# A two-layer decoder trunk on one core: column units and down steps of the FFN laid out anew

## The chip, the cores and the metric

The kernel runs on one core of one Trainium2 chip. The metric is the device time of one execution in microseconds (us); lower is better. One core has five engines that are spoken of below: PE (TensorE, matrix products), DVE (VectorE), ACT (ScalarE), POOL (GpSimd) and SP, which here only issues DMA transfers, in the order in which they are written. Each engine works through its own instructions in order and waits on semaphores for the others.

## The reference

Two layers over a stream of 1024 tokens by 1024 features, all in float32. Layer 0 is a gated DeltaNet mixer, layer 1 a stick-breaking attention; each is followed by the same feed-forward network (FFN), and it is in the FFN that the change lies:

```
def swiglu(x, w_gu, w_down):
    g, u = jnp.split(x @ w_gu, 2, axis=-1)
    return (jax.nn.silu(g) * u) @ w_down

for layer in range(DEPTH):                       # DEPTH = 2, D_FF = 2816
    hn = rms_norm(h, attn_norm[layer])
    h = h + (gdn_mixer if layer == 0 else sb_mixer)(hn, ...)
    h = h + swiglu(rms_norm(h, ffn_norm[layer]), w_gu[layer], w_down[layer])
```

## The kernel before

The program runs the mixer of layer 0 (to about 700 us), its FFN (to about 1430), the attention (to about 1930) with its output projection, and the second FFN (from about 1975 to the end). Both FFNs are made by one function, `ffn`.

**Precision and products.** Every float32 operand is held as two parts, hi (the value cast by ACT) and lo (the rest, by a DVE subtraction); `parts_of` makes both (L359 the cast, L360 the subtraction). A product is then three matmuls (`triple`, L450 hi by hi, L451 hi by lo, L452 lo by hi). On top of that the FFN multiplies 2x2 blocks with seven products instead of eight, which needs sums and differences of blocks on both sides and of the results. The seven products of an item are numbered 1 to 7, and `Seven.steps` runs one.

**Column units.** The 2816 hidden columns are 22 units of 128. A unit's left sides are its gate and up weights; its right sides are the normed activations X, kept by `PairNorm` as four column blocks (j = 0 to 3) under the names 11, 21, 22, T1 to T4. `PairNorm.half` makes 11 and 21 from the first half of the tokens; `second(j)` makes T1 = second-half row minus raw, and T2 from it, each with its parts (two ACT copies L407, two DVE subtractions L408 and L409, then `parts`); `side5`, `side347` and `side4` make T1's parts, T3 and 22, and T4's parts later. The units' results are combined by `c11`, `u2`, `u3`, `c21`, `c12` (L525 to L549; L537 is ACT's copy in `u3`, L548 the Silu and L549 POOL's last multiply).

**Pairs and DRAM.** Two units make a pair (11 pairs, q = 0 to 10). `sums(q)` forms the pair's left sides for the down projection: four POOL sums (L578, L579, L582, L583), hi by ACT and lo by DVE (L586, L587, and L558, L559 in `split_put`), and stores them to DRAM, `hsa[q]` and `hsb[q]`, by `put` (L552). It is a generator that is advanced once at every product step of PE.

**Down steps.** 24 blocks, four (row groups c) for each of six groups gi; group 0 is pair 0 alone and takes four plain products (11, 21, 12, 22), the others two pairs and seven products. A block reads its left sides back from DRAM by `hid_load` (hA from `hsa` into four buffers of tag w, L664 for group 0, L669 else; hB from `hsb`, L676). `Right` makes a pair's right sides from `w_down`: `load` (L630, three raw buffers), `sums` (POOL, L638 to L641), `split` (parts). `rows_load` fetches the residual rows h (L682). What is done beside each product is set by hand in `beside_unit` and `beside_block`; the numbers of the steps there (s, k) are the order of the work. Results go into h by L718.

Of the kernel before, what the change touches and what calls it, by code (L numbers as in the profile page):

```python
# [18 lines left out]
P = 128  # L19
# [4 lines left out]
def yoco_kernel(  # L24
# [338 lines left out]
    class PairNorm(Norm):  # L363
# [36 lines left out]
        def second(self, j):  # L400

            rr = [x_tile(F32), x_tile(F32)]
            t1 = x_tile(F32)
            t2 = x_tile(F32) if j < 3 else main.tile([P, HB], F32, tag="og", name="t2")
            for k, r in enumerate(rr):
                kt = 4 * k + j
# [4 lines left out]
            self.tt = getattr(self, "tt", []) + [(*rr, t1, t2)]  # L411

        def side5(self, j):
            self.parts("T1", j, self.tt[j][2])

        def side347(self, j):
            r12, r22, _, t2 = self.tt[j]
            dve.tensor_tensor(r12, r22, r12, op=ALU.subtract)
            self.parts("T3", j, r12)
            dve.tensor_tensor(t2, self.raw[4 + j], t2, op=ALU.subtract)  # L420
            self.parts("22", j, r22, self.x2)

        def side4(self, j):
            self.parts("T4", j, self.tt[j][3])
# [29 lines left out]
    def ffn(norm, rows, w_gu, w_down, hp, done, after=None, sizes=(1, 2, 2, 2, 2, 2)):  # L454
# [119 lines left out]
        def sums(q):  # L574

            v = [hid.pop(2 * q + k) for k in range(2)]
            s = W()
            pool.tensor_tensor(s[:, 0], v[0][:, :, 1], v[1][:, :, 1], op=ALU.add)  # L578
            pool.tensor_tensor(s[:, 1], s[:, 0], v[0][:, :, 0], op=ALU.subtract)  # L579
            yield  # L580
            v3, v4 = v[0][:, :, 1], main.tile([P, 4, P], F32, tag="og", name="s4")
            pool.tensor_tensor(v3, v[0][:, :, 0], v3, op=ALU.subtract)  # L582
            pool.tensor_tensor(v4, v[1][:, :, 0], s[:, 1], op=ALU.subtract)  # L583
# [4 lines left out]
            yield  # L588
            yield
            for k in range(2):  # L590
                put(hsa[q], 2 + k, hi[:, k].bitcast(F32))
                put(hsa[q], 6 + k, s[:, k])
            yield from split_put(hsa[q], 0, 4, *(t[:, :, 0] for t in v))
            yield
            yield
            yield from split_put(hsb[q], 0, 3, v3, v[1][:, :, 1])
            yield
            yield from split_put(hsb[q], 2, 5, v4)
            yield
# [19 lines left out]
        class Right:  # L619


            def __init__(self, gi, q):
                self.gi, self.q, self.w = gi, q, {}
                wd[gi][q] = self.w

            def load(self):
                self.r = [raw_tile([P, 2, HB]) for _ in range(2)]
                for k in range(2):
                    r0 = (2 * self.q + k) * P
                    sp.dma_start(self.r[k].rearrange("p a b -> p (a b)"), w_down[r0 : r0 + P, :])  # L630
# [134 lines left out]
        def beside_unit(i, s):  # L765
# [47 lines left out]
        def beside_block(b, s):  # L813
            gi, c = divmod(b, 4)
            if gi == 0:
                k = 6 + 4 * (c - 1) + s if c else s
                if k == 2:
                    pend.append(sums(NPAIR - 1))
                if s == 0:
                    if c < 3:  # L820
                        rows_load(c + 1)
                    hid_load(b + 1)
                if k == 0:
                    right(1, 0, "split", 7)
                elif k == 1:
                    right(1, 0, "split", 3, 4)
                    right(1, 1, "load")
                elif k == 3:
                    right(1, 1, "sums")
                elif k in (5, 7, 9, 11, 13, 15, 16):  # L830
# [44 lines left out]
        u2.split_g()  # L875
        run_.step(0, 6)
        for j in range(4):
            norm.side5(j)
        run_.step(1, 6)
        for u, k in ((u0, 0), (u1, 1)):  # L880
            u.c11(run_.bank[k, "A"])
        u0.split34()
        run_.step(2, 1)
        run_.step(0, 5)
        u1.split34()
        for j in range(4):
            norm.side347(j)
# [839 lines left out]
```

## Time and profile before

| | us |
|---|---|
| runs | 2680.41, 2686.52, 2685.96 |
| median of the runs | 2685.96 |
| profiled execution, its own time | 2682.77 |
| its span in the profile | 2681.0 |
| granted TensorE clock, mean | 0.987 |

The profiled execution is the one whose rows are shown below. Its time is 1.8 us more than its span, and 3.2 us less than the median of the three runs. Busy time counts an engine's instructions; PE's matmuls overlap, so PE is told best by when one starts after the other. A group of waits names the instruction that waited and the one that released it last. Line numbers are those of the kernel before.

### The profile page before, as it was taken

The page shows a single profiled execution, that of the slowest core. Times are in us where ns is not written, and L with a number is a line of the kernel's source. Part 1 is how long each engine was busy: PE and PEld are TensorE (multiplying, and loading weights), DVE is VectorE, ACT ScalarE, POOL GpSimd, SP SyncE. Part 2 cuts the span into 40 slices and gives each one's busy share as a digit, 9 for nine tenths or more (in the row PEclk, how much of TensorE's full clock was granted, in tenths as well). Part 3 has the DMA queues.
Part 4 walks back from the last instruction along what each step waited for, and adds up shares of the span by engine and source line. Part 5 has one row for each costly group of instructions (what it writes and reads, how often), then busy time and mean ns, then how long its engine had stood idle before and what let it go on. Part 6 is the DMA issues. An engine that isn't in the chain of part 4 may idle for free. (4 is left out here: it accounts for less than half of the span.)

```text
span 2681.0 us, 35748 instructions
## 1 busy us (share of the span) xinstructions
PE 2550.9 (95%) x12908; PEld 2078.1 (78%) x12908; DVE 1820.2 (68%) x2715; ACT 1143.9 (43%) x2207; POOL 825.1 (31%) x1248
## 2 busy tenths in 40 slices
PE   8999999999989999979999999999899999996999
PEld 6777877877768888857777778887777888885777
DVE  6666776675685666657755788778668566664874
ACT  6333333343463444432215666667545444442220
POOL 2444444443401222234313333332410221223420
PEclk9999999999999999989999999999999999998999
DMA  4222222222423554477661111111333445547765
GB/s 121 65 62 57 55 65 53 72 92 72 145 84 109 169 157 143 144 245 276 232 216 63 40 32 32 40 40 63 111 118 102 128 142 163 164 143 258 244 230 200
DMA packets 368374, 331.75 MB, mean 124 GB/s; under 512 B 19507, under 2 KB 320702, under 8 KB 368198
## 3 DMA queue, kind: packets, MB, share of 16 engines
q1 hardware_dynamic: 368198, 329.48, 38.8%
q8 instruction: 101, 1.65, 0.2%
q14 instruction: 75, 0.61, 0.1%
HBM read 226.37 MB, written 103.06 MB: 123 GB/s over the span
## 5 line engine op out<-in xcount | busy, mean ns | idle before, releaser
L140 PE MATMUL ups<-x,wh 128*128 128x512 f32 (+1 forms) x912 | 388.7, 427 | 0.0
L142 PE MATMUL ups<-x,wl 128*128 128x512 f32 (+1 forms) x912 | 363.6, 399 | 0.0
L141 PE MATMUL ups<-x,wh 128*128 128x512 f32 (+1 forms) x912 | 359.7, 395 | 0.0
L450 PE MATMUL ips<-x,w 128*128 128x512 f32 x840 | 328.1, 392 | 15.3 <-ACT x L359 9.3
L451 PE MATMUL ips<-x,w 128*128 128x512 f32 x840 | 328.7, 391 | 2.7 <-DVE x L360 2.5
L452 PE MATMUL ips<-x,w 128*128 128x512 f32 x840 | 327.9, 390 | 0.0
L549 POOL TENSOR_TENSOR n<-n,ev 128x512 f32<-128x512 f32 x44 | 68.8, 1564 | 695.3 <-ACT n L548 695.3
L450 PE MATMUL ups<-x,w 128*128 128x512 f32 x648 | 253.6, 393 | 1.7 <-ACT x L359 1.7
L451 PE MATMUL ups<-x,w 128*128 128x512 f32 x648 | 253.8, 392 | 0.0
L452 PE MATMUL ups<-x,w 128*128 128x512 f32 x648 | 253.2, 391 | 0.0
L142 PEld LDWEIGHTS ups<-x,wl 128*128 128x128 f32 (+1 forms) x912 | 170.9, 187 | 37.5
L450 PEld LDWEIGHTS ips<-x,w 128*128 128x128 f32 x840 | 157.4, 188 | 53.3 <-ACT x L359 11.9
L140 PEld LDWEIGHTS ups<-x,wh 128*128 128x128 f32 (+1 forms) x912 | 172.2, 189 | 22.7
L141 PEld LDWEIGHTS ups<-x,wh 128*128 128x128 f32 (+1 forms) x912 | 172.2, 189 | 21.2
L451 PEld LDWEIGHTS ips<-x,w 128*128 128x128 f32 x840 | 157.9, 188 | 37.7 <-DVE x L360 4.9
L452 PEld LDWEIGHTS ips<-x,w 128*128 128x128 f32 x840 | 158.0, 188 | 32.9
L718 DVE TENSOR_TENSOR h<-h,ips 128x512 f32<-128x512 f32 x176 | 119.4, 683 | 68.8 <-PE ips L452 68.8
L450 PEld LDWEIGHTS ups<-x,w 128*128 128x128 f32 x648 | 122.5, 189 | 28.7 <-ACT x L359 3.3
L451 PEld LDWEIGHTS ups<-x,w 128*128 128x128 f32 x648 | 122.5, 189 | 26.8 <-DVE x L360 1.6
L452 PEld LDWEIGHTS ups<-x,w 128*128 128x128 f32 x648 | 122.2, 189 | 25.4
L718 DVE TENSOR_TENSOR h<-h,ups 128x512 f32<-128x512 f32 x136 | 92.7, 682 | 58.4 <-PE ups L452 58.3
L360 DVE TENSOR_TENSOR w<-raw,w 128x1024 fp32r<-128x1024 f32 (+1 forms) x88 | 101.0, 1163 | 40.8 <-DMA hsb<-w 31.5
(351 smaller groups left out, 5935.5 us busy)
## 6 DMA issues: line engine op xcount, KB each, us to landing
raw<-in_ffn_w_gu_dram SPq DMA_DIRECT2D x88, 512.0 KB, 3.9
w<-hsa SPq DMA_DIRECT2D x88, 512.0 KB, 4.2
hsa<-w SPq DMA_DIRECT2D x128, 256.0 KB, 2.8
hb<-hsb SPq DMA_DIRECT2D x72, 384.0 KB, 4.1
raw<-in_ffn_w_down_dram SPq DMA_DIRECT2D x44, 512.0 KB, 3.8
raw<-in_gdn_w_in_dram SPq DMA_DIRECT2D x32, 512.0 KB, 4.1
hsb<-w SPq DMA_DIRECT2D x60, 256.0 KB, 3.7
hsa<-n SPq DMA_DIRECT2D x48, 256.0 KB, 3.6
```

The costliest lines, as they stand in the source:

```text
L140: pe.matmul(o, wh[:, kt, :m], xh, start=kt == 0, stop=False)
L141: pe.matmul(o, wh[:, kt, :m], xl, start=False, stop=False)
L142: pe.matmul(o, wl[:, kt, :m], xh, start=False, stop=kt == KT - 1)
L360: dve.tensor_tensor(lo, src, hi, op=ALU.subtract)
L450: pe.matmul(ps, ah, bh, start=start, stop=False, skip_group_check=True)
L451: pe.matmul(ps, ah, bl, start=False, stop=False, skip_group_check=True)
L452: pe.matmul(ps, al, bh, start=False, stop=stop, skip_group_check=True)
L549: pool.tensor_tensor(s, s, self.t3, op=ALU.mult)
L718: dve.tensor_tensor(d, d, ps, op=ALU.add)
```

## The change

Four things change, in `PairNorm` and `ffn`.

- **Start-up.** `second(j)` takes t1 and t2 straight from PSUM by two DVE instructions that multiply by the gain and subtract (new L406, L407). Of the two ACT copies only that of the row block 22 (`r22`) is left. T3 is formed as t2 minus raw, in a tile of its own. `behind` is the last lo part of T2 (new L411), and `issue_after` orders on DVE everything from u2's split to `side347` behind it; `u1.split34` moves between the columns of `side347`.
- **Pair sums.** `sums(q)` casts and subtracts its halves apart (512 wide) and stores hi, lo, hi, lo. For the last pair its tiles are ten small ones, its lo subtractions are POOL's instead of DVE's (new L602), and it begins four steps later (k = 6 instead of 2).
- **Loads.** The right sides' halves are loaded apart and earlier; `hid_load` for blocks 0 to 4 and `rows_load` move to other steps, so that those of blocks 0 to 3 stand ahead of the last pair's stores. In block 4 the load for block 5 moves from s = 1 to s = 5.
- **Splits.** Group 1's first pair is split in another order (5 and 7 later by a step, 3 and 4 too).

```diff
 def second(self, j):
-    rr = [x_tile(F32), x_tile(F32)]
...
-        act.activation(r, self.columns(self.hn, kt), AF.Copy, scale=self.gain[:, kt : kt + 1])
-    dve.tensor_tensor(t1, rr[0], self.raw[j], op=ALU.subtract)
-    dve.tensor_tensor(t2, rr[1], t1, op=ALU.subtract)
-    self.parts("T2", j, t2)
+    p12, p22 = self.columns(self.hn, j), self.columns(self.hn, 4 + j)
...
+    dve.scalar_tensor_tensor(t1, p12, g(j), self.raw[j], op0=ALU.mult, op1=ALU.subtract)
+    dve.scalar_tensor_tensor(t2, p22, g(4 + j), t1, op0=ALU.mult, op1=ALU.subtract)
+    act.activation(r22, p22, AF.Copy, scale=g(4 + j))
+    hi, lo = x_tile(), x_tile()
+    act.copy(hi, t2)
+    self.behind = dve.tensor_tensor(lo, t2, hi, op=ALU.subtract)

 def side347(self, j):
-    dve.tensor_tensor(r12, r22, r12, op=ALU.subtract)
-    self.parts("T3", j, r12)
+    t3 = x_tile(F32)
+    dve.tensor_tensor(t3, t2, self.raw[j], op=ALU.subtract)
+    self.parts("T3", j, t3)

 def sums(q):
-    s = W()
+    last = q == NPAIR - 1
+    w = None if last else W()
+    s = [small(), small()] if last else [w[:, 0], w[:, 1]]
...
-    hi = mw()
-    act.copy(hi, s)
-    dve.tensor_tensor(s, s, hi, op=ALU.subtract)
+    for n, (dst, k0, k1, srcs) in enumerate(todo):
+        if last:
+            his = [small(F32R) for _ in srcs]
...
+        for hi, src in zip(his, srcs):
+            act.copy(hi, src)
+            (pool if last else dve).tensor_tensor(src, src, hi, op=ALU.subtract)
...
+        for k, (hi, src) in enumerate(zip(his, srcs)):
+            put(dst, k0 + k, hi.bitcast(F32))
+            put(dst, k1 + k, src)

 def beside_unit(i, s):
-    if i == NF - 2 and s == 6:
-        right(0, 0, "load")
+    if i == NF - 2 and s in (1, 6):
+        right(0, 0, "load", int(s == 6))
     if i == NF - 1:
         if s == 0:
+            right(1, 0, "load", 0)
+        elif s == 1:
             right(0, 0, "sums")
             right(0, 0, "split", 11, 12)
         elif s == 2:
             right(0, 0, "split", 21, 22)
-            right(1, 0, "load")
+            right(1, 0, "load", 1)
+        elif s == 3:
+            rows_load(0)
         elif s == 4:
             hid_load(0)
-            rows_load(0)
             right(1, 0, "sums")
         elif s == 5:
+            hid_load(1)
             right(1, 0, "split", 1, 2)
         elif s == 6:
-            right(1, 0, "split", 6, 5)
+            rows_load(1)
+            right(1, 0, "split", 6)

 def beside_block(b, s):
-        if k == 2:
-            pend.append(sums(NPAIR - 1))
-        if s == 0:
-            if c < 3:
-                rows_load(c + 1)
-            hid_load(b + 1)
         if k == 0:
+            hid_load(2)
+            right(1, 0, "split", 5)
+        elif k == 1:
             right(1, 0, "split", 7)
-        elif k == 1:
+            right(1, 1, "load")
+        elif k == 2:
+            rows_load(2)
+            hid_load(3)
             right(1, 0, "split", 3, 4)
-            right(1, 1, "load")
         elif k == 3:
             right(1, 1, "sums")
+        elif k == 6:
+            rows_load(3)
+            pend.append(sums(NPAIR - 1))
+        elif k == 10:
+            hid_load(4)
...
-        if s == 1:
+        if s == (5 if b == 4 else 1):
             hid_load(b + 1)

+with tc.issue_after(norm.behind.ins):
     u2.split_g()
...
```

**What moves, first place: DVE at the start-up** (first FFN; x, t and w are tiles of activations, of t2 and of weights). Before, from the first column's L408 on:

```order
L408 TENSOR_TENSOR x<-x,x_7517 128x512
L360 TENSOR_TENSOR w<-w 128x1024
L409 TENSOR_TENSOR x<-x 128x512
L360 TENSOR_TENSOR w<-w 128x1024
L418 TENSOR_TENSOR x<-x 128x512
L360 TENSOR_TENSOR x<-x 128x512
L360 TENSOR_TENSOR w<-raw,w 128x1024
L408 TENSOR_TENSOR x<-x,x_7528 128x512
L420 TENSOR_TENSOR x<-x_7602,x 128x512
L409 TENSOR_TENSOR x<-x 128x512
L360 TENSOR_TENSOR x_7951<-x,x_7950 128x512
```

And now, from the first column's lo part on:

```order
L411 TENSOR_TENSOR x<-x 128x512
L406 SCALAR_TENSOR_TENSOR x<-ips,gains,x_7528 128x512
L407 SCALAR_TENSOR_TENSOR x<-ips,gains,x 128x512
L411 TENSOR_TENSOR x<-x 128x512
L406 SCALAR_TENSOR_TENSOR x<-ips,gains,x_7556 128x512
L407 SCALAR_TENSOR_TENSOR x<-ips,gains,x 128x512
L411 TENSOR_TENSOR x<-x 128x512
L406 SCALAR_TENSOR_TENSOR x<-ips,gains,x_7576 128x512
L407 SCALAR_TENSOR_TENSOR t_7832<-ips,gains,x 128x512
L411 TENSOR_TENSOR x<-t_7832,x 128x512
L360 TENSOR_TENSOR w<-raw,w 128x1024
L360 TENSOR_TENSOR x<-x 128x512
```

Before, a column's two subtractions had weight splits (L360, 1024 wide) and the T1 and T3 work of earlier columns (L418, L420) between them. Now each column is two instructions and its lo part, and all other work stands behind the fourth.

**Second place: SP at the down start** (first FFN; `hsa_7379` is pair 0, `hsa_7389` and `hsb_7400` the last pair, h the residual rows). Before, from the load of block 2's left sides to that of block 3's:

```order
L664 DMA w_11092<-hsa_7379 128x1024
L552 DMA hsa_7389<-w_11075 128x4x128
L552 DMA hsa_7389<-n_10735 128x4x128
L552 DMA hsa_7389<-w_11075 128x4x128
L552 DMA hsa_7389<-n_10902 128x4x128
L552 DMA hsb_7400<-w_11118 128x4x128
L552 DMA hsb_7400<-n_10735 128x4x128
L552 DMA hsb_7400<-w_11118 128x4x128
L552 DMA hsb_7400<-n_10902 128x4x128
L682 DMA h_11150<-hmid_7294 128x1024
L682 DMA h_11152<-hmid_7294 128x1024
L664 DMA w_11154<-hsa_7379 128x1024
```

And now, from behind block 2's load to the first load of block 4, which reads pair 1, `hsa_7380`:

```order
L643 DMA raw_11017<-in_ffn_w_down_dram 128x1024
L643 DMA raw_11019<-in_ffn_w_down_dram 128x1024
L695 DMA h_11036<-hmid_7294 128x1024
L695 DMA h_11038<-hmid_7294 128x1024
L677 DMA w_11040<-hsa_7379 128x1024
L695 DMA h_11092<-hmid_7294 128x1024
L695 DMA h_11094<-hmid_7294 128x1024
L555 DMA hsa_7389<-x_11123 128x4x128
L555 DMA hsa_7389<-x_11096 128x4x128
L555 DMA hsa_7389<-x_11124 128x4x128
L555 DMA hsa_7389<-x_11097 128x4x128
L682 DMA w_11159<-hsa_7380 128x1024
```

Before, block 2's load had four stores of the last pair ahead of it, and block 3's eight more. Now the loads of blocks 0 to 3 are ahead of all these stores, and block 4's first load stands behind four of them, with two rows of h ahead of those.

**Third place: POOL at the down start** (first FFN). Before, from the multiply of unit 20 on:

```order
L549 TENSOR_TENSOR n<-n,ev 128x512
L638 TENSOR_TENSOR w<-raw 128x512
L640 TENSOR_TENSOR w<-raw 128x512
L639 TENSOR_TENSOR w<-raw,w 128x512
L641 TENSOR_TENSOR w<-raw,w 128x512
L549 TENSOR_TENSOR n<-n,ev 128x512
L578 TENSOR_TENSOR w<-n 128x512
L638 TENSOR_TENSOR w<-raw 128x512
L579 TENSOR_TENSOR w<-w,n 128x512
L639 TENSOR_TENSOR w<-raw,w 128x512
L640 TENSOR_TENSOR w<-raw 128x512
L641 TENSOR_TENSOR w<-raw,w 128x512
```

And now, the same place (L651 to L654 are L638 to L641, L552 is the multiply, L585 and L586 are L578 and L579):

```order
L651 TENSOR_TENSOR w<-raw 128x512
L652 TENSOR_TENSOR w<-raw,w 128x512
L653 TENSOR_TENSOR w<-raw 128x512
L654 TENSOR_TENSOR w<-raw,w 128x512
L552 TENSOR_TENSOR n<-n,ev 128x512
L651 TENSOR_TENSOR w<-raw 128x512
L653 TENSOR_TENSOR w<-raw 128x512
L652 TENSOR_TENSOR w<-raw,w 128x512
L654 TENSOR_TENSOR w<-raw,w 128x512
L552 TENSOR_TENSOR n<-n,ev 128x512
L585 TENSOR_TENSOR x<-n 128x512
L586 TENSOR_TENSOR x<-x,n 128x512
```

Before, group 1's first four right-side sums stood behind the multiply of unit 20 (the first L549), and the second four among the last pair's sums. Now each four stand ahead of the multiply, unit 20's and unit 21's. Behind the last row now follow the last pair's other two sums (L588, L589) and seven subtractions (L602) that were DVE's; before, its other two sums follow.

## Rows read from the trace of the kernel before

**Rows 1.** The page, part 1: busy time, share of the span, instructions.

```profile
PE 2550.9 (95%) x12908; PEld 2078.1 (78%) x12908; DVE 1820.2 (68%) x2715; ACT 1143.9 (43%) x2207; POOL 825.1 (31%) x1248
```

**Rows 2.** Waits of PE, whole span; columns: total us, times, longest.

```profile
PE ups L450 <- DMA w<-hsa: 34.1, 4, 14.2
PE ips L450 <- ACT x L359: 9.3, 6, 1.9
...
PE ips L450 <- ACT ev L537: 6.0, 2, 3.2
```

**Rows 3.** Timeline of PE, down start of the first FFN: start, duration, instruction, idle before.

```profile
1164.48 0.39 PE L452 MATMUL ups<-wd,w 128*128 128x512 f32 x1
1167.67 0.50 PE L450 MATMUL ips<-x,w 128*128 128x512 f32 x1 [2.80 <-ACT ev L537]
...
1175.74 0.39 PE L452 MATMUL ips<-wd,w 128*128 128x512 f32 x1
...
1182.54 0.39 PE L452 MATMUL ups<-wd,w 128*128 128x512 f32 x1
...
1195.46 0.76 PE L450 MATMUL ups<-wd,w 128*128 128x512 f32 x1 [12.54 <-DMA w<-hsa]
...
1206.86 0.47 PE L450 MATMUL ups<-wd,w 128*128 128x512 f32 x1 [3.30 <-DMA w<-hsa]
...
1214.00 0.39 PE L450 MATMUL ips<-x,w 128*128 128x512 f32 x1
```

**Rows 4.** The same of the second FFN.

```profile
2427.23 0.39 PE L452 MATMUL ups<-wd,w 128*128 128x512 f32 x1
...
2460.21 0.77 PE L450 MATMUL ups<-wd,w 128*128 128x512 f32 x1 [14.16 <-DMA w<-hsa]
...
2479.69 0.39 PE L450 MATMUL ips<-x,w 128*128 128x512 f32 x1
```

**Rows 5.** Windows of 5 us, first FFN: busy time by engine, PEclk, DMA share, GB/s.

```profile
1195.00:1200.00 5.00, 4.54 (x11) 3.60 (x12) 4.43 (x7) 0.00 (x0) 0.28 (x1) 0.50 1.14 340
```

**Rows 6.** Timeline of SP, its DMA issues, down start of the first FFN.

```profile
1189.98 0.91 SPq L552 DMA_DIRECT2D hsa<-w  x2
1190.99 0.51 SPq L664 DMA_DIRECT2D w<-hsa  x1
...
1200.41 0.44 SPq L664 DMA_DIRECT2D w<-hsa  x1
```

**Rows 7.** Timeline of POOL, the same place.

```profile
1157.47 1.36 POOL L549 TENSOR_TENSOR n<-n,ev 128x512 f32<-128x512 f32 x1 [15.19 <-ACT n L548]
...
1177.89 1.30 POOL L578 TENSOR_TENSOR w<-n 128x512 f32<-128x512 f32 x1
...
1181.63 1.75 POOL L639 TENSOR_TENSOR w<-raw,w 128x512 f32<-128x512 f32 x1
```

**Rows 8.** Timeline of ACT, the same place.

```profile
1167.05 0.57 ACT L537 COPY ev<-ips 128x512 f32<-128x512 f32 x1
```

**Rows 9.** Waits of PE, 745 to 770 us, start-up of the first FFN.

```profile
PE ips L450 <- ACT x L359: 4.7, 3, 1.9
PE ips L451 <- DVE x L360: 1.3, 2, 1.0
```

**Rows 10.** Timeline of DVE, the same start-up: the last lo part of T2.

```profile
764.84 0.68 DVE L360 TENSOR_TENSOR x<-t,x 128x512 fp32r<-128x512 f32 x1
```

**Rows 11.** Windows of 5 us of that start-up, columns as in Rows 5.

```profile
765.00:770.00 5.00, 5.00 (x13) 3.87 (x12) 4.04 (x7) 3.45 (x8) 0.00 (x0) 0.50 0.01 2
```

**Rows 12.** Lines by form: DVE product-and-subtract from PSUM, ACT scaled copy (count, busy, mean ns).

```profile
L1295 DVE SCALAR_TENSOR_TENSOR og<-ips,og_half,sz 128x512 f32<-128x512 f32 x16 | 12.0, 751 | 7.6 <-PE ips L1092 7.4
...
L407 ACT ACTIVATE x<-ips,gains 128x512 f32<-128x512 f32 x16 | 10.3, 684 | 0.0
```

**Rows 13.** Timeline of DVE: a lo part taken while POOL works.

```profile
1187.09 1.74 DVE L559 TENSOR_TENSOR n<-n,w 128x512 f32<-128x512 f32 x1 [4.26 <-POOL n L582]
```

**Rows 14.** DMA issues, 1140 to 1220 us: count, KB each, median us to landing.

```profile
raw<-in_ffn_w_down_dram SPq DMA_DIRECT2D x7, 512.0 KB, 6.0
```

More of the change, by code (lines that the diff above doesn't have):

```diff
@@ L400, in second @@
         def second(self, j):
-            rr = [x_tile(F32), x_tile(F32)]
-            t1 = x_tile(F32)
+            g = lambda kt: self.gain[:, kt : kt + 1]
+            p12, p22 = self.columns(self.hn, j), self.columns(self.hn, 4 + j)
+            t1, r22 = x_tile(F32), x_tile(F32)
             t2 = x_tile(F32) if j < 3 else main.tile([P, HB], F32, tag="og", name="t2")
-            for k, r in enumerate(rr):
-                kt = 4 * k + j
-                act.activation(r, self.columns(self.hn, kt), AF.Copy, scale=self.gain[:, kt : kt + 1])
-            dve.tensor_tensor(t1, rr[0], self.raw[j], op=ALU.subtract)
-            dve.tensor_tensor(t2, rr[1], t1, op=ALU.subtract)
-            self.parts("T2", j, t2)
-            self.tt = getattr(self, "tt", []) + [(*rr, t1, t2)]
+            dve.scalar_tensor_tensor(t1, p12, g(j), self.raw[j], op0=ALU.mult, op1=ALU.subtract)
[4 more added lines that the diff above has]
+            self.behind = dve.tensor_tensor(lo, t2, hi, op=ALU.subtract)
+            self.X["T2"][j] = hi, lo
+            self.tt = getattr(self, "tt", []) + [(r22, t1, t2)]
         def side5(self, j):
-            self.parts("T1", j, self.tt[j][2])
+            self.parts("T1", j, self.tt[j][1])
         def side347(self, j):
-            r12, r22, _, t2 = self.tt[j]
-            dve.tensor_tensor(r12, r22, r12, op=ALU.subtract)
-            self.parts("T3", j, r12)
+            r22, _, t2 = self.tt[j]
+            t3 = x_tile(F32)
+            dve.tensor_tensor(t3, t2, self.raw[j], op=ALU.subtract)
+            self.parts("T3", j, t3)
             dve.tensor_tensor(t2, self.raw[4 + j], t2, op=ALU.subtract)
@@ L423, in side4 @@
         def side4(self, j):
-            self.parts("T4", j, self.tt[j][3])
+            self.parts("T4", j, self.tt[j][2])
     class Seven:
@@ L574, in sums @@
         def sums(q):
+            last = q == NPAIR - 1
             v = [hid.pop(2 * q + k) for k in range(2)]
-            s = W()
-            pool.tensor_tensor(s[:, 0], v[0][:, :, 1], v[1][:, :, 1], op=ALU.add)
-            pool.tensor_tensor(s[:, 1], s[:, 0], v[0][:, :, 0], op=ALU.subtract)
+            small = lambda dt=F32: x_tile(dt).rearrange("p (c x) -> p c x", x=P)
+            w = None if last else W()
+            s = [small(), small()] if last else [w[:, 0], w[:, 1]]
+            v3, v4 = v[0][:, :, 1], small() if last else main.tile([P, 4, P], F32, tag="og", name="s4")
@@ L586, in sums @@
-            act.copy(hi, s)
-            dve.tensor_tensor(s, s, hi, op=ALU.subtract)
[L588 to L598, printed above, removed]
@@ L599, in sums @@
-            yield
+            todo = [(hsa[q], 2, 6, s), (hsa[q], 0, 4, [t[:, :, 0] for t in v]), (hsb[q], 0, 3, [v3, v[1][:, :, 1]]),
+                    (hsb[q], 2, 5, [v4])]
+            for n, (dst, k0, k1, srcs) in enumerate(todo):
+                if last:
+                    his = [small(F32R) for _ in srcs]
+                else:
+                    hi = mw()
+                    his = [hi[:, k] for k in range(len(srcs))]
+                for hi, src in zip(his, srcs):
+                    act.copy(hi, src)
+                    (pool if last else dve).tensor_tensor(src, src, hi, op=ALU.subtract)
+                yield
+                if n == 0 or last:
+                    yield
+                for k, (hi, src) in enumerate(zip(his, srcs)):
+                    put(dst, k0 + k, hi.bitcast(F32))
+                    put(dst, k1 + k, src)
+                if n:
+                    yield
+                if n == 1:
+                    yield
@@ L622, in __init__, with load @@
             def __init__(self, gi, q):
-                self.gi, self.q, self.w = gi, q, {}
+                self.gi, self.q, self.w, self.r = gi, q, {}, {}
                 wd[gi][q] = self.w
-            def load(self):
-                self.r = [raw_tile([P, 2, HB]) for _ in range(2)]
-                for k in range(2):
+            def load(self, *ks):
+                for k in ks or (0, 1):
+                    self.r[k] = raw_tile([P, 2, HB])
                     r0 = (2 * self.q + k) * P
@@ L874, in ffn @@
         run(both)
[L875 to L887, printed above, removed]
+        with tc.issue_after(norm.behind.ins):
+            u2.split_g()
+            run_.step(0, 6)
+            for j in range(4):
+                norm.side5(j)
+            run_.step(1, 6)
+            for u, k in ((u0, 0), (u1, 1)):
+                u.c11(run_.bank[k, "A"])
+            u0.split34()
+            run_.step(2, 1)
+            run_.step(0, 5)
+            for j in range(4):
+                norm.side347(j)
+                if j == 1:
+                    u1.split34()
         run_.step(1, 5)
```

7 lines of the change are left out of this document (4 added, 3 removed).

## The prediction

> **What bounds the kernel now.** I began with the busy times on the page. PE is busy 95% of the span, DVE 68%, ACT 43% and POOL 31% [rows 1], and the number of products does not change. So the change can only win where PE stands idle or runs at a lower clock, and lose where it makes PE wait anew. The next view is therefore PE's list of waits [rows 2]. Its first line is a DMA that brings left sides back from DRAM: 34.1 us in only 4 waits. The third line, 6.0 us in 2 waits, is for ACT's copy in `u3`. The second, 9.3 us in 6 waits, is mostly the start-up. Then the timeline of PE tells where these sit. All of the DMA waits are at the first down steps, two in each FFN: 12.54 us ahead of block 2 and 3.30 us ahead of block 3 in the first [rows 3], 14.16 us for block 2 in the second [rows 4]; 4.1 of the 34.1 are left for its block 3. The wait for `u3` stands just ahead of them, 2.80 us in the first FFN [rows 3].
>
> The reason for the DMA waits is on SP. The load of block 2's left sides was issued at 1190.99, right behind two stores of the last pair at 1189.98, and that of block 3 at 1200.41, behind eight more stores [rows 6]. The data of pair 0 had been in DRAM long before. The stores wait for sums that POOL made from 1177.89 on [rows 7] and for the hi and lo parts after them, and everything behind them on the one queue waits too.
>
> **Term 1, the down start.** What could the stretch take without waits? In the first FFN the last matmul ahead of the first wait starts at 1164.48 and the first one of block 4 at 1214.00 [rows 3]; 114 matmuls lie from the end of that wait up to block 4. Between 1175.74 and 1182.54 there are 30 steps from one start to the next, 0.227 us each, at full clock. So 114 take 25.85 us, and 1214.00 - 1164.48 - 0.23 - 25.85 = 23.4 us is lost. The same from 2427.23 to 2479.69 in the second [rows 4] gives 26.4 us. Together 49.8 us, of which 40.1 are the idle time of the first and third lines of [rows 2]; the rest is matmuls at a granted clock of 0.50, which is the 1.2 GHz level, after PE had been idle (1195 to 1200 us shows it, with 11 matmuls in 5 us, [rows 5]).
>
> In the new order the loads of blocks 0 to 3 stand ahead of all stores of the last pair. What then stands ahead of block 3's load on SP are loads and the stores of the pair before, which are ready by about 1162, as I estimate from the stretch in which the old SP was issuing the same stores. With the slowest landing of the two loads seen, 1200.41 to 1206.86 [rows 3, 6], 6.45 us, it is there at about 1169. PE, with no wait behind it, needs block 2 at 1164.71 + 66 x 0.227 = 1179.7 and block 3 at 1185.1. So 16 us are in hand. The two waits for `u3` should go too: ACT came to that copy at 1167.05 [rows 8], because it took casts of the right sides first that waited for POOL's sums, and these were queued behind a multiply at 1157.47 that waited 15.19 us for ACT [rows 7]. Now the four sums stand ahead of that multiply, and ACT has fewer casts ahead of the copy. I take the whole: **-49.8 us**. If the `u3` waits stayed it would be 6.0 less.
>
> **Term 2, the start-up.** PE waits 6.0 us there in the first FFN [rows 9], and then runs 13 matmuls from 765 to 770 at clock 0.50 [rows 11] where 22 fit: 9 x 0.227 = 2.0 us more. So at most 8 us in each FFN can be won, 16 in all. Before, a column of T2 took an ACT copy, then another, two DVE subtractions with other work between, a cast and a lo part. Now it takes two DVE instructions from PSUM, and then the cast and the lo part. No row shows the new form here, but the nearest, a product with PSUM and another operand on 128x512, takes 0.751 us, against 0.684 for the ACT copy that goes [rows 12]. A column then costs DVE 2 x 0.75 + 0.68 = 2.2 us, and 3.3 to 3.5 us with the casts between, as a chain. Before, the last lo part of T2 ran at 764.84 [rows 10]; four such columns from about 746 on (an estimate, four old columns of 4.7 us back from that row) put it at 757 to 760. The price is that all of DVE's other work stands behind it: some 27 instructions of 0.60 us pitch and three wide ones of 1.2 us, about 20 us of backlog (0.60 is what one after another takes on DVE by my reading, a little under the 0.68 of [rows 10]), from which T3's last lo part comes at about 775, where PE would like it at about 773. So I leave PE 2 us of waits for T2's last column and 2 us for T3, against 6.0, and let part of the slow clock go: about -3 us in each FFN, **-6 us**. The ends are -8 in each if all waits go, and +3 in each if the backlog costs PE 5 us more than I think; I stay in the middle because either queue is DVE's and its work is the same.
>
> **Term 3, what is late next.** Block 4 now is reached at 1164.71 + 25.85 = 1190.6 instead of 1214, and its loads stand behind the last pair's first four stores. These wait for POOL: the second half of the right sides should land at about 1166 (issue near 1160, 6.0 us to land, [rows 14]), and then come 11 POOL instructions (four right sums, the multiply, four sums, two of the seven subtractions that it takes from DVE). At 1.3 us each, the common time [rows 7], they end at 1180.5; at 1.6, between that and the 1.75 of one in that row, at 1183.9. With 1 us for issue and 4.5 to 6.45 us to land [rows 3, 6], block 4's left sides come between 1186.0 and 1191.4, against 1190.6. Block 5's follow five more subtractions and are needed at about 1198. So the margin is about nil, and I charge 2 us in each FFN, **+4 us**; the ends are 0 and the first rival.
>
> The halved sums of the other pairs cost ACT 2 x 0.62 for 1.05 us, and DVE about the same; both engines have idle time in that stretch, so it costs nothing, and if that cover were gone 0.2 us for each pair, 2 us for each FFN. The seven subtractions taken off DVE are in no chain of PE's but POOL's, above.
>
> **The sum.** 2682.8 - 49.8 - 6 + 4 = 2631.0 us. This is against the profiled execution's own time, which is 3.2 us under the median of the three runs shown; a median of the changed kernel can stand some 3 us higher.
>
> **The rivals.**
>
> *The wait moves on to blocks 4 to 7.* POOL and DVE can get in each other's way. One lo part on DVE took 1.74 us while POOL was at work [rows 13], where another of the same size took 0.68 with POOL idle [rows 10, 11]. If each of the 11 POOL instructions has to give way for one such DVE instruction, it takes 1.29 + 0.68 = 1.97 us, the chain ends at 1188.0, and block 4's data lands at 1193.5 to 1195.4. That is 3 to 5 us of waiting, about 2 us at the lower clock behind it, and up to 5 us more at block 5: 5 to 12 us in each FFN. Against it: POOL's own rows here are 1.30 and 1.75, not 1.97. The time would be 2682.8 - 49.8 - 6 + 10 to 24, or **2637 to 2651**. The Trainium skill, page "SBUF — State Buffer", section "Who interferes with whom", says that DVE and GpSimd share one pair of ports as an exclusive lock, so that a DVE instruction with two SBUF inputs and a GpSimd instruction block each other in full. The trace agrees in part: the 1.74 is what such a block would look like on DVE, and by that rule the sum itself would be this rival's.
>
> *The start-up gate starves PE.* If T1's and T3's parts, held back behind T2, come 8 us late instead of 2 in each FFN, term 2 turns from -6 to +6: **2643**. For it speaks that DVE is already busy 4.04 of 5 us there [rows 11]; against it that PE has other products at hand first.
>
> *Slower.* The same POOL chain decides, at block 4: if it is so stretched that block 4 starts later than the 1214.00 of before [rows 3], the change loses. That point is (1214 - 6.45 - 1 - 1166) / 11 = 3.7 us for each POOL instruction, twice the longest seen [rows 7]. At 5 us each it is 14.7 us later in each FFN: 2682.8 + 29 - 6 = **2706**. Nothing in the rows comes near that price.
>
> *The waits stay.* SP may stop at a row of h or a left-side buffer that is not free, ahead of block 3's load. It would take 16 us of that to reach PE, and as much as before to give the old time: **2677 to 2683**.
>
> **How the numbers follow.** About 0.3% (8 us) is what a measurement of this kernel can tell from no change. The forecast with its own spread (2617 to 2637) gets 0.68, the first rival 0.16, the start-up gate 0.06, the waits that stay 0.05, slower 0.05. The range reaches down to all of both terms, 2682.8 - 49.8 - 16 = 2617, and up to the first rival with its upper price and the 3 us of the median, 2655. Faster by over 0.3% is the sum of the first three, 0.90; within 0.3% is 0.05, slower 0.05.
>
> **What would show it.** In the profile after, the line of waits for the DMA from `hsa` should fall from 34.1 to under 8 us, that for `u3` be gone, and block 4's first matmul come some 26 us after the last one of unit 21's stretch before it, with the clock near full from there. At the start-up T2's last lo part should come by 760 where it was 764.84, and PE's waits be about 4 us. The prediction is wrong if block 4 or 5 shows waits over 3 us each, if POOL's instructions take near 2 us, or if waits of PE for DVE behind T2 grow beyond 6 us.

## The result, and the profile after

The changed kernel takes 2653.8 us (median of 4 runs, 2649.92 to 2657.28) beside 2684.0 us for the kernel before in the same job (4 runs): a ratio of 0.989, 95% interval 0.987 to 0.991. It is some 30 us faster, where the forecast had 51.8 (from the profiled execution's 2682.77 to 2631.0): inside the stated range, and close to its upper end. The profiled execution of the changed kernel took 2657.28 us, the slowest of its four, so between the two profiled executions the gain is 25.5 us.

The page's first part, which answers to [rows 1]:

```profile
PE 2544.3 (96%) x12908; PEld 2071.8 (78%) x12908; DVE 1840.7 (69%) x2721; ACT 1143.8 (43%) x2219; POOL 859.2 (32%) x1262
```

PE is busy 6.6 us less for the same instructions: it ran less at the lower clock (mean granted clock 0.992, 0.987 before). POOL has 34 us more, DVE 20 us more.

The waits of PE over the whole span (total us, times, longest), which answer to [rows 2]:

```profile
PE ips L453 <- DMA w<-hsa: 14.2, 5, 5.6
PE ips L453 <- DVE h L731: 10.4, 13, 1.5
...
PE ups L453 <- DVE h L731: 2.9, 3, 1.6
```

The DMA waits have fallen from 34.1 to 14.2 us but not to the 8 at most that the prediction named. They have moved: the matmuls that wait now write `ips`, at blocks 4 and 5, where those of blocks 2 and 3 wrote `ups`. The wait for ACT's copy in `u3` is below 0.5 us in both FFNs. What has grown are PE's waits for L731, DVE's sums into h (L718 before): 13.3 us in 16 times, up to 1.6 us at a time; before, that was 4.8 us in 12 times of at most 0.6.

PE's timeline at the first FFN's down start, as in [rows 3] (start, duration, instruction, idle before):

```profile
1158.84 0.39 PE L455 MATMUL ups<-wd,w 128*128 128x512 f32 x1
1159.07 0.39 PE L453 MATMUL ips<-x,w 128*128 128x512 f32 x1
...
1175.79 0.50 PE L453 MATMUL ups<-wd,w 128*128 128x512 f32 x1 [1.61 <-DVE h L731]
...
1187.00 0.50 PE L453 MATMUL ips<-x,w 128*128 128x512 f32 x1
...
1189.96 0.47 PE L453 MATMUL ips<-wd,w 128*128 128x512 f32 x1 [2.00 <-DMA w<-hsa]
...
1202.88 0.79 PE L453 MATMUL ips<-x,w 128*128 128x512 f32 x1 [5.56 <-DMA w<-hsa]
```

The `u3` wait (before 1159.07) is gone. Block 2 starts at 1175.79 without any DMA wait, but 1.61 us late for DVE. Block 4 starts at 1187.00 where it was 1214.00, and then PE waits 2.00 us for the second half of its left sides, and 5.56 us at block 5. Set the n-th matmul of the FFN in the one profile against the n-th in the other, and the gain of the first FFN's down start is seen to swell and shrink: 21.4 us at block 4's first matmul (1214.00 to 1187.00, less the 5.6 us that it is ahead by the last row before the `u3` wait, 1.0 of them from before the FFN), 11.6 a block later, and 9.0 some 65 us later, where it stays. In the second FFN 11.2 us are left. So of the 23.4 and 26.4 us that the prediction found lost, 14.4 and 15.2 are still lost, in other places. The start-ups gained 4.6 us each.

SP's issues there, as in [rows 6] (the x2 or x4 at a row's end is how many transfers it sums up):

```profile
1175.27 6.87 SPq L555 DMA_DIRECT2D hsa<-x  x4
1182.23 0.60 SPq L682 DMA_DIRECT2D w<-hsa  x1
...
1184.70 0.59 SPq L555 DMA_DIRECT2D hsa<-x  x1
...
1188.39 2.44 SPq L555 DMA_DIRECT2D hsb<-x  x1
...
1193.41 2.24 SPq L555 DMA_DIRECT2D hsb<-x  x2
1195.70 1.06 SPq L643 DMA_DIRECT2D raw<-in_ffn_w_down_dram  x2
1196.85 0.40 SPq L682 DMA_DIRECT2D w<-hsa  x1
```

And POOL, as in [rows 7]:

```profile
1164.81 1.29 POOL L651 TENSOR_TENSOR w<-raw 128x512 f32<-128x512 f32 x1 [9.57 <-PE ups L455]
...
1178.74 3.02 POOL L602 TENSOR_TENSOR x<-x 128x512 f32<-128x512 f32 x2
1181.71 5.05 POOL L602 TENSOR_TENSOR n<-n,x 128x512 f32<-128x512 f32 x4
```

POOL's chain went as the sum had it: it began the right-side sums at 1164.81, and from there to the second of the lo subtractions (1178.74 and 3.02 more) are 11 instructions in 17 us, 1.54 each. (The row at 1164.81 names PE as what ended the wait; the same instruction of the second FFN, at 2419.47, names the load from `w_down`.) The last three of the first four stores stood behind it, and block 4's load was issued at 1182.23, where 1181.5 to 1185 was forecast. What was not forecast comes next. Ten more stores stand on SP from 1184.70 to 1195.65, 1.1 us each in the mean; then two right-side loads; and only then, at 1196.85, block 5's left sides, which PE needed at 1197.3. It got them at 1202.88, 6.0 us after that issue. POOL had finished at 1188.0. The fourth of the ten stores waited for it until then; the six behind it, from 1188.39, waited for no engine that the profile shows and still took 1.2 us each. So it was mainly SP and the DMA engines behind it that held block 5's load. The windows say so (busy time by engine, PEclk, DMA share, GB/s):

```profile
1190.00:1195.00 5.00, 5.00 (x22) 4.16 (x23) 2.06 (x3) 0.00 (x0) 0.00 (x0) 1.00 1.14 343
1195.00:1200.00 5.00, 2.32 (x10) 1.52 (x9) 0.00 (x0) 0.00 (x0) 0.00 (x0) 0.95 1.11 374
1200.00:1205.00 5.00, 2.12 (x5) 1.73 (x6) 4.04 (x5) 2.37 (x4) 4.50 (x3) 0.50 1.02 412
```

The DMA share is 1.0 and more from 1190 to 1205, while DVE, ACT and POOL do nothing from 1195 to 1200; PE is idle for 5.56 us up to 1202.88, and its clock is 0.50 in the window from 1200.

### The profile page after: what moved, and what is told of

Read it like the earlier page. It is cut to its first block, busy times and chain, and to the rows that moved or that the text cites. A ratio compares the mean times of both kernels' runs of the same rounds, so it can differ in the third digit from the quotient of the medians.

```text
span 2655.6 us, 35824 instructions
## 1 busy us (share of the span) xinstructions
PE 2544.3 (96%) x12908; PEld 2071.8 (78%) x12908; DVE 1840.7 (69%) x2721; ACT 1143.8 (43%) x2219; POOL 859.2 (32%) x1262
## 5 line engine op out<-in xcount | busy, mean ns | idle before, releaser
L552 POOL TENSOR_TENSOR n<-n,ev 128x512 f32<-128x512 f32 x44 | 71.2, 1618 | 623.8 <-ACT n L551 623.8
L731 DVE TENSOR_TENSOR h<-h,ips 128x512 f32<-128x512 f32 x176 | 119.3, 682 | 68.9 <-PE ips L455 68.7
L454 PEld LDWEIGHTS ups<-x,w 128*128 128x128 f32 x648 | 121.8, 188 | 26.4 <-DVE x L360 1.2
L731 DVE TENSOR_TENSOR h<-h,ups 128x512 f32<-128x512 f32 x136 | 92.2, 682 | 45.9 <-PE ups L455 45.7
L104 DVE TENSOR_TENSOR wl<-raw,wh 128x1024 fp32r<-128x1024 f32 x64 | 82.3, 1287 | 57.6 <-ACT wh L103 57.4
```

What stands on the lines that cost most here:

```text
L104: dve.tensor_tensor(lo, raw, hi, op=ALU.subtract)
L454: pe.matmul(ps, ah, bl, start=False, stop=False, skip_group_check=True)
L552: pool.tensor_tensor(s, s, self.t3, op=ALU.mult)
L731: dve.tensor_tensor(d, d, ps, op=ALU.add)
```

## The experiments

All ratios are to the kernel before, run in the same job; its median was between 2681.7 and 2684.3 us in the four jobs, so versions of different jobs are compared by their ratios. Gains of a place are read as above, matmul by matmul, between two profiles.

**The two parts alone.** First the kernel before with the start-up part only (`second`, `side347`, `side5`, `side4` and the order behind T2), then the changed kernel with that part undone.

> The kernel before with the start-up part of the change alone (T1 and T2 from PSUM, DVE's other work behind T2). If the two parts of the change are independent, each FFN's start-up gives what the two profiles show between the same matmuls, 4.6 and 4.7 us, so about 2684 - 9 = 2675 us, and PE's four waits for the left sides from DRAM stay at 34 us in all. If the gain at the start-up were only work put off to later, the time would be within 3 us of the kernel before.

> The changed kernel with the start-up part undone: only the loads, buffers and sums at the down start. By the same profiles the down starts give 9.0 and 11.2 us: about 2664 us, if the parts are independent. Waits of PE for hsa stay at some 14 us in 4 or 5 times, as in the changed kernel.

Measured: 2673.97 us, ratio 0.9965 (0.9949 to 0.9981), and 2664.52 us, ratio 0.9921 (0.9904 to 0.9938), beside 2684.3. The gains are 10.3 and 19.8 us, and their sum 30.1 is the whole change's 30.2: the parts add up, within the 4 to 5 us that each interval leaves open. In the first run the four waits at blocks 2 and 3 stay, 33.9 us (one of them is put down to DVE there); in the second, the waits for `hsa` are 15.2 us, near the whole change's 14.2.

**The order of loads undone.** The changed kernel with the last pair's sums begun at k = 2 again, with blocks 2 and 3 loaded behind its first four and eight stores, and with block 4's loads at k = 14 instead of 10:

```diff
                 if k == 0:
-                    hid_load(2)
...
                     rows_load(2)
-                    hid_load(3)
+                    pend.append(sums(NPAIR - 1))
...
                     rows_load(3)
-                    pend.append(sums(NPAIR - 1))
+                    with tc.issue_after(puts[-1].ins):
+                        hid_load(2)
                 elif k == 10:
+                    with tc.issue_after(puts[-1].ins):
+                        hid_load(3)
+                elif k == 14:
                     hid_load(4)
```

> The changed kernel with the last pair's sums begun four steps earlier again and the loads of blocks 2 and 3 behind its first four and first eight stores on SP, as before the change; all else as in the change. Theory of SP's queue: block 2 waits for stores that end about 1182 and a landing of 4.5 us, some 11 us where the changed kernel has none, and block 3 after it; blocks 4 and 5 then have their data in time: 2665 to 2680 us. Rival, the gain of the down start came from the right sides and the halved sums and not from the order of the loads: 2650 to 2658 us.

Measured: 2652.41 us, ratio 0.9894 (0.9878 to 0.9911): no slower than the changed kernel. PE's wait for block 2 and SP's issues:

```profile
1184.59 0.76 PE L453 MATMUL ups<-wd,w 128*128 128x512 f32 x1 [11.90 <-DMA w<-hsa]
...
1172.80 6.87 SPq L557 DMA_DIRECT2D hsa<-x  x4
1179.72 0.54 SPq L679 DMA_DIRECT2D w<-hsa  x1
```

The wait that the change was seen to remove is back in full, 11.90 us (12.54 in [rows 3]) and 11.75 us in the second FFN, and yet the time is the same, since no wait of PE behind it in that stretch is over 0.7 us. The theory had the waits right and the time wrong; the rival had the time right. The order of the loads and the later begin of the sums do place the wait, but with the rest of the change in, placing it costs or gains nothing: PE waits at block 2, or at blocks 4 and 5. The last pair's stores are through SP at 1190.3 in this run and at 1195.7 in the changed kernel, whose PE is only 1.5 us later at the end of the units. What part of the change gives the down starts their 20 us is not told apart here. What the rows show is that the first four of the stores are through at 1179.7 in this run, where they were at 1190.9 before [rows 6], while PE is 7.1 us ahead at the end of the units.

**The subtractions back on DVE.**

```diff
-                    (pool if last else dve).tensor_tensor(src, src, hi, op=ALU.subtract)
+                    dve.tensor_tensor(src, src, hi, op=ALU.subtract)
```

> The changed kernel with the last pair's seven lo subtractions back on DVE. Theory of SP's queue: block 4's loads come 2 to 4 us earlier and its wait of 2.0 us goes, but block 5's loads still stand behind ten stores and two right-side loads, so its wait of 5.6 us stays: 2648 to 2652 us. Rival, POOL's chain is the limit: the waits of blocks 4 and 5 both go, 2636 to 2642 us. Third: DVE, already late for the h sums in this stretch, gets later, and PE's waits for L731 grow: over 2654 us.

Measured: 2647.44 us, ratio 0.9865 (0.9850 to 0.9879), 0.6 us under the range of the theory of SP's queue. Beside the changed kernel's 0.989 the two intervals still overlap a little; by the profiles each down start gains 3.6 us on the changed kernel's. PE at block 5, SP, and DVE's first two subtractions:

```profile
1200.06 0.78 PE L453 MATMUL ips<-x,w 128*128 128x512 f32 x1 [3.52 <-DMA w<-hsa]
...
1175.29 3.19 SPq L555 DMA_DIRECT2D hsa<-x  x3
1178.58 0.46 SPq L682 DMA_DIRECT2D w<-hsa  x1
...
1193.88 0.40 SPq L682 DMA_DIRECT2D w<-hsa  x1
...
1176.32 1.77 DVE L602 TENSOR_TENSOR x<-x 128x512 f32<-128x512 f32 x1 [0.56 <-POOL x L586]
...
1179.29 0.69 DVE L602 TENSOR_TENSOR x<-x 128x512 f32<-128x512 f32 x1 [0.60 <-POOL x L589]
```

Block 4's first load is issued 3.65 us earlier (1178.58 for 1182.23) and its wait is gone; block 5's load is issued at 1193.88 for 1196.85, and its wait is 3.52 us for 5.56 (4.27 for 4.52 in the second FFN). So POOL's chain had a part in block 5's wait in the first FFN, and the larger part is left without it. A wait for the h sums of some 1.5 us is new at block 3, as the third expectation had it, but smaller than what is gained. What POOL took over in the change was a cost: 7 instructions of 1.3 us and more ahead of the stores on which block 4 waits, taken from an engine that needs 0.68 for one, and 1.77 for the first, which runs beside POOL.

**Block 5's loads ahead.** First together with the third group's right sides (loaded at k = 11), then without them (block 5's hA alone at k = 13); `hid_load` takes the part that it is to load, and block 5's hB follows at s = 1 of block 4.

```diff
+                elif k == 11:
+                    right(2, 0, "load")
+                elif k == 14:
+                    hid_load(5, "A")
...
-                    hid_load(b + 1)
+                    hid_load(b + 1, "B" if b == 4 else "AB")
```

> The changed kernel with the loads of the third group's first right sides and block 5's hA put ahead of the last pair's later stores on SP (hsa's second four and all of hsb), block 5's hB behind them. Theory of SP's queue: block 5's wait (5.6 and 4.5 us) goes with the 0.50 clock behind it, and part of the waits for DVE some 40 us later, since the right sides come some 10 us earlier: 12 to 20 us less, 2634 to 2642 us. Rival, POOL's chain: block 5's wait stays, 2650 to 2654 us. Rival, the transfers themselves are at their limit there (DMA share 1.0): the wait moves to block 4 or hB, 2646 to 2652 us.

> The changed kernel with block 5's hA alone moved ahead of most of the last pair's hsb stores. It tells the left sides apart from the right sides that were moved with them in the run before. Theory: the 7.4 and 8.1 us waits there were DVE held up by the right sides that came late, so without them block 5's waits (5.6 and 4.5 us) and about 1 us of low clock each go: 2641 to 2646 us. Rival, whatever comes first on the full DMA engines only delays the next: 2650 to 2655 us.

Measured: 2656.7 us, ratio 0.9895 (0.9880 to 0.9910), and 2649.1 us, 0.9876 (0.9861 to 0.9891). The first is a miss, with a new wait of PE, followed here back to DVE and ACT:

```profile
1197.18 0.79 PE L453 MATMUL ips<-x,w 128*128 128x512 f32 x1 [7.44 <-DVE h L735]
...
1190.22 1.27 DVE L360 TENSOR_TENSOR x<-raw,x 128x512 fp32r<-128x512 f32 x1 [8.88 <-ACT x L359]
1191.42 0.67 DVE L735 TENSOR_TENSOR h<-h,ips 128x512 f32<-128x512 f32 x1
...
1189.57 0.62 ACT L359 CAST x<-raw 128x512 fp32r<-128x512 f32 x1 [12.30 <-DMA raw<-in_ffn_w_down_dram]
```

The casts of the right sides waited for their data until 1189.57 (their loads had been issued at 1181.87, onto full DMA engines), the lo part on DVE waited for the cast for 8.88 us, and since the scheduler had put that lo part ahead of the h sums, these waited too, and PE with them: 7.44 us. The second keeps the right sides where they were: block 5's wait falls from 5.56 to 1.20 us and from 4.52 to 2.09, but the h sums come later (waits of 2.5 and 1.7 us in the first FFN), so of the 8 to 13 us expected some 3 are left, by the ratios and by the profiles, which the spread of the runs does not tell from nothing. The time lies between the two expectations.

**Both, and block 4's loads earlier.** The subtractions on DVE, block 5's hA at k = 13, and block 4's loads at k = 8 instead of 10. By then the DMA engines have room: the share is 0.05 from 1170 to 1175 in the changed kernel.

```diff
+                if k == 8:
+                    hid_load(4)
+                if k == 13:
+                    hid_load(5, "A")
```

> The changed kernel with the last pair's subtractions on DVE, block 4's loads ahead of the last pair's first stores, and block 5's hA ahead of most of its hsb stores; the right sides of the third group stay where the change has them, so that nothing new stands ahead of the h sums on DVE. Theory of SP's queue: of the waits left in the run with the subtractions on DVE, those of block 5 (3.5 and 4.3 us) go with the low clock behind them: 2636 to 2642 us. Rival, the DMA engines are the limit in that stretch (share 1.0): the wait moves to block 5's hB or to the next right sides, 2644 to 2650 us.

Measured: 2640.39 us, ratio 0.9847 (0.9832 to 0.9861). PE's waits and SP:

```profile
PE ips L453 <- DVE h L735: 11.8, 13, 2.5
...
1168.01 0.32 SPq L684 DMA_DIRECT2D w<-hsa  x1
...
1174.41 3.21 SPq L555 DMA_DIRECT2D hsa<-x  x2
1177.71 0.46 SPq L684 DMA_DIRECT2D w<-hsa  x1
...
1183.34 0.82 SPq L684 DMA_DIRECT2D w<-hsa  x1
```

No wait for `hsa` is left in PE's list of the stretch. Only the first of block 4's two hA went out ahead of all stores, at 1168.01, released by PE; the second went out at 1177.71, behind two stores, and was still in time. What is left is the h sums on DVE.

**The start-up without the order behind T2.**

```diff
-        with tc.issue_after(norm.behind.ins):
+        if True:
             u2.split_g()
```

> The changed kernel without the order on DVE behind the last lo part of T2, T1 and T2 still from PSUM. If the form from PSUM is what shortens the chain, 2652 to 2657 us. If the order makes it (wide weight splits of 1.2 us and T1's parts kept out from between the columns), most of the 10 us of the start-up is lost: 2660 to 2664 us.

Measured: 2644.93 us, ratio 0.9864 (0.9850 to 0.9879): faster by more than either expected. DVE in the changed kernel at the first L406 and around the last two columns, and the same without the order (whose FFN starts 2.95 us earlier in its profile):

```profile
739.97 0.75 DVE L406 SCALAR_TENSOR_TENSOR x<-ips,gains,x 128x512 f32<-128x512 f32 x1 [1.33 <-PE ips L379]
...
751.99 0.69 DVE L411 TENSOR_TENSOR x<-x 128x512 fp32r<-128x512 f32 x1 [1.26 <-ACT x L410]
...
755.45 0.69 DVE L411 TENSOR_TENSOR x<-t,x 128x512 fp32r<-128x512 f32 x1 [1.26 <-ACT x L410]
```

```profile
737.02 0.75 DVE L406 SCALAR_TENSOR_TENSOR x<-ips,gains,x 128x512 f32<-128x512 f32 x1 [1.33 <-PE ips L379]
...
751.29 0.69 DVE L411 TENSOR_TENSOR x<-x 128x512 fp32r<-128x512 f32 x1
...
752.56 0.69 DVE L360 TENSOR_TENSOR w<-raw,w 128x512 fp32r<-128x512 f32 x1
...
755.17 0.69 DVE L411 TENSOR_TENSOR x<-t,x 128x512 fp32r<-128x512 f32 x1 [1.26 <-ACT x L410]
```

With the order, DVE stands idle for 1.26 us in each of the last three columns, for ACT's cast, since only the column's own work may stand there. Without it only the last column has that gap; in the others weight splits and combines stand there. From the first L406 to T2's last lo part are 15.5 us with the order and 18.2 without, so the order does shorten the chain, by 2.7 us. But PE gains nothing by it: with the order it waits 1.54 us for the last column and then 1.1 us more, near 775, for parts that are late behind it; without, it waits 1.8 us for earlier columns and for nothing after. The start-up gains 8.0 and 7.2 us instead of 4.6 each. That is 5.9 us in all by the profiles, beside 6.4 by the two ratios.

**All together, and the right sides once more.** The first run joins the last two experiments. The second loads the third group's first right sides at k = 8, the third run at k = 12, and in both every later group's first lo parts are ordered behind the h sum before them:

```diff
                     hid_load(4)
+                    right(2, 0, "load")
...
-                    right(gi + 1, 0, "split", SIDES[k - 6])
+                    with tc.issue_after(added[0].ins):
+                        right(gi + 1, 0, "split", SIDES[k - 6])
```

> The run with block 4's and block 5's loads ahead of the stores and the subtractions on DVE, and now also without the order on DVE behind T2. If what the two experiments gained at different places adds, 2640.4 less some 6 us of the start-up (3.0 and 2.6 us by the progress of PE in the run without that order): 2633 to 2636 us. Rival: work that is put off at the start-up comes back at the units behind it, 2639 to 2642 us.

> The same, and the third group's first right sides loaded ahead of the last pair's first stores, with their lo parts on DVE ordered behind the h sums that stand before them in the program (as they did not in the run that first moved this load). Theory: the waits of PE for the h sums that are left at the blocks behind block 5 (2.5 and 1.8 us in the first FFN, 1.9 and 1.5 in the second, with low clock behind them) come from these parts being bunched on DVE after a late load, and go: 2626 to 2631 us. Rival: DVE waits for the load at the head of its queue again, 2640 us and more.

> As the run before it, but the third group's first right sides are loaded behind the last pair's hsa stores and ahead of block 5's hA, so that POOL's sums of them come some 10 us later, after DVE has taken the last pair's lo parts. Theory: the 3.8 and 3.9 us waits for the h sums at block 3 in the run before came from POOL and DVE at work at once, and go; those behind block 5 stay small: 2630 to 2635 us. Rival: the right sides land later on full DMA engines and the parts bunch up again, 2636 to 2642 us.

Measured: 2636.25 us (ratio 0.9831, 0.9814 to 0.9848), 2641.58 us (0.9847, 0.9832 to 0.9862), 2634.67 us (0.9835, 0.9817 to 0.9853). The first is the sum of the parts within its spread. The second is a miss: the waits in the 50 us behind block 5 fall under 0.9 us as foreseen, but two of 3.8 and 3.9 us come at block 3, where POOL now works on these right sides at the time that DVE has the last pair's lo parts:

```profile
1181.69 0.80 PE L453 MATMUL ups<-wd,w 128*128 128x512 f32 x1 [3.78 <-DVE h L737]
...
1175.58 1.29 POOL L651 TENSOR_TENSOR w<-raw 128x512 f32<-128x512 f32 x1
...
1175.65 1.77 DVE L602 TENSOR_TENSOR x<-x 128x512 f32<-128x512 f32 x1 [0.59 <-POOL x L589]
```

That lo part took 1.77 us. With the load some 10 us later (the third run) the longest of these waits is 2.3 us, and its time is the first one's again. Either beats both kernels; the changed one by 15 and 14 us by the ratios. What is left is DVE, as PE's waits of the third run show, the last row one of its longest:

```profile
PE ips L453 <- DVE h L737: 12.0, 18, 2.2
...
PE ups L453 <- DVE h L737: 5.3, 3, 2.3
...
1291.10 0.50 PE L453 MATMUL ips<-wd,hb 128*128 128x512 f32 x1 [2.15 <-DVE h L737]
```

This wait, with one of 2.17 us in the second FFN, is new in the second and third runs: at the same matmul neither the changed kernel nor the first run waits as much as 0.2 us. The order behind the h sums, which those two runs put on all later groups, is the likely cause; no run has the earlier load without it.

## Why the prediction was right, and where it was off

The direction and the places were right; the sum was not. 2631.0 and the forecast's own spread, 2617 to 2637, which had a chance of 0.68, were missed by 23 and 17 us. The stated range holds the measured time only because it was drawn up to the first rival's upper price and 3 us more, so the number is partly luck. One of the signs that were to show it wrong came too: block 5's waits are 5.56 and 4.52 us, over the 3 named.

**Term 1** (-49.8 us at the two down starts) was right in what it saw and wrong in what it took as gained by it. The waits for `u3` went (5.5 us of idle time), and so did those at blocks 2 and 3, which the term put down to the order on SP. But it took their whole length as gained once the loads were ahead. The run with the order undone shows that this order, with the later begin of the sums, was worth nothing measurable: 11.9 us come back at block 2, and the 11 us of waits that the changed kernel has from block 2 to block 8 of the first FFN go. The term should have asked when the loads of blocks 4 and 5, which stand behind the stores, are through. Where these too were put ahead, with the subtractions on DVE, the waits for `hsa` did go.

**Term 3** (+4 us, what is late next) is the one that was mis-sized. It had the right place, and block 4's load to the microsecond (issue 1182.23, wait 2.00 us in either FFN). For block 5 it counted five more POOL instructions and found the margin about nil; it did not count the ten stores and two loads that stand ahead of block 5's load on SP, which take from 1184.70 to 1196.8, though it had named just that queue as the cause of the waits before. Its own rows had the price: between the two loads of [rows 6] stand eight stores and two rows of h, some 0.9 us each, at a DMA share of 1.14 in [rows 5]. Nor did it price the h sums: 13.3 us of PE's waits over the span, where the trace of before had 4.8. Measured in place of 2 us in each FFN: 14.4 and 15.2.

**Term 2** (-6 us) measured -10.3 alone and -9.2 between the profiles. T2's last lo part came at 755.45, where 757 to 760 was expected. The waits left were 2.6 us in the first FFN where 4 was taken. That the rest of DVE's work comes late behind the order was named, with a price; it was not seen that the order need not be there.

**The first rival** (the wait moves on to blocks 4 to 7, 2637 to 2651 us) is what happened, 3 us outside its time. Its cause was named half right: POOL's instructions took 1.54 us each, not 1.97. The larger share, block 5's, was SP and the DMA engines: with the subtractions off POOL 3.52 of its 5.56 us were left, and with its load moved ahead of the hsb stores 1.20. The loss, 14.4 and 15.2 us, is also more than the 5 to 12 that the rival named.

**The rule weighed.** POOL and DVE beside it in two places of the changed kernel:

```profile
1171.67 0.67 DVE L731 TENSOR_TENSOR h<-h,ips 128x512 f32<-128x512 f32 x1
1172.27 1.19 DVE L360 TENSOR_TENSOR wd<-w,wd 128x512 fp32r<-128x512 f32 x1
...
1171.16 1.74 POOL L552 TENSOR_TENSOR n<-n,ev 128x512 f32<-128x512 f32 x1
...
1177.48 1.86 DVE L360 TENSOR_TENSOR x<-w,x 128x512 fp32r<-128x512 f32 x1 [1.14 <-ACT x L359]
...
1177.49 1.30 POOL L589 TENSOR_TENSOR x<-n,x 128x512 f32<-128x512 f32 x1
```

L731 has one of its inputs in PSUM and takes its usual 0.67 us beside a POOL instruction; the lo part next to it, both inputs in SBUF, takes 1.19, and POOL's own 1.74. The Trainium skill, page "SBUF — State Buffer", section "Who interferes with whom", has it so, that a DVE instruction with two SBUF inputs contends with a GpSimd instruction that reads SBUF, and that whoever issues first keeps the shared pair while the other waits. The trace agrees: at 1177.49 POOL takes its usual 1.30 us and the lo part beside it 1.86; POOL's 1.29 at 1164.81 began ahead of the lo part beside it; and the four subtractions from 1181.71, with only h sums beside them, take 1.30 each. So not every POOL instruction pays, and one that does took up to 1.76 us in this chain, not the 1.97 of the rival's sum.

Left open: the profile of the changed kernel lost 5.3 us to the one of before between the two FFNs, where no instruction moved. The eleven other profiles lose between 0.5 and 4.7 us there. That all twelve lose against this one profile may mean that it was quick there; it is not explained.

## What to carry to other kernels

A wait in front of which a queue is reordered is gained only if nothing later waits for the same queue's end: before crediting it, follow the whole burst to its last transfer, count the issues at their price under load (here 1.1 us each with the DMA engines full, 0.4 without), and see when the next consumer needs its data. An order that keeps other work out of a chain is worth its price only if what is held back is needed later than the chain: here the chain came 2.7 us sooner, and PE lost 3.4 and 2.5 us. Moving work to a free engine can lengthen a chain if that engine is slower at it and others wait for its data.

## What was not expected of the hardware

With the DMA share at 1.0, a store's issue on SP took some 1.2 us (six that waited for no engine, from 1188.39 to 1195.65, between 0.64 and 2.44 each), against 0.37 for the first store of the last pair, at 1175.27, with the share at 0.17. And a lo part on DVE took between 1.17 and 1.86 us beside POOL in the changed kernel from 1165 to 1180, and 0.69 at 757.20 with POOL idle, so a mean over a whole kernel does not price it.
